# Branch-b merge gates as two sets of seven block products among the GLA key and query tiles

## The chip, the cores and the metric

One core of a Trainium2 chip runs one program. The metric is device time in microseconds (us), the median of several runs; a separate profiled run gives the trace. Engines: PE (TensorE: matmuls and transposes), ACT (ScalarE), DVE (VectorE), POOL (GpSimd) and SP (SyncE, which here only issues transfers). Weights come from DRAM by 16 DMA engines that all queues share.

## The reference, cut to what matters

256 tokens, width 2048, one layer, batch 1, all in fp32:

```python
h = rmsnorm(x, pre_norm_g)
proj = h @ w_in                     # 2048 x 18448
(a_q, a_k, a_v, a_g, a_lr, b_q, b_k, b_v, b_g, m_a, m_b) = split(proj)
gk  = log_sigmoid(a_lr @ gla_gk_w2 + gla_gk_b) / 16
o_a = rmsnorm(gla_chunked(a_q, a_k, a_v, gk), gla_norm_g) * silu(a_g)
o_b = rmsnorm(diff_attention(b_q, b_k, b_v, lam), diff_norm_g) * 0.8 * silu(b_g)
y_a, y_b = o_a @ w_branch_a, o_b @ w_branch_b
merged = sigmoid(m_a) * y_a + sigmoid(m_b) * y_b
return x + rmsnorm(merged @ w_out, post_norm_g)
```

a_q and a_k have 1024 columns, a_lr 16, all others 2048. The change is about m_b, a product of 256 x 2048 by 2048 x 2048 whose result goes through a sigmoid, and about what runs near it.

## The kernel before, in words

**Splits.** An fp32 product is made from rounded parts. Each weight tile `raw` is loaded by SP (L142) in chunks of 128 x 2048 (1 MB), and each half of it (128 x 1024) is rounded by ACT into `hi` (L161); DVE makes `lo = raw - hi` (L162). The activations have been split in the same way into `xs` (L197, L198). PE then makes three passes: x_hi w_hi, x_lo w_hi, x_hi w_lo. `raw`, `hi` and `lo` have three buffers each (L87), and `take` (L167) has halves emitted four ahead (AHEAD). So a load waits until a buffer is free, which is when DVE's `lo` has read it.

**Tiles.** The tokens are 2 blocks of 128, K is 16 tiles of 128. `token_major` (L308, matmul L322) makes 512 columns for both blocks: 16 x 2 x 3 = 96 matmuls of 512 columns, in 8 halves of 12. `channel_major` (L333) makes a k or q tile of 128 channels, in 2 halves: 16 matmuls of 512 (L343, both x parts beside one another) and 16 of 256 (L345).

**Order.** `chunk_plan` (L32) sets the order of the weights, and so that of the work: values v0 to v4, GLA keys and queries (k0, q0, k1, q1; four tiles each), GLA output gates ag0 to ag3, difference heads 0 and 1, then four times a merge gate of branch a and its branch product (m0g, y0g), heads 2 and 3, the four merge gates of branch b (m1g, L744), y1 (four), and the output product o (four). All engines' instructions are put in order at build time, under the data's dependencies.

**Tasks.** Smaller work is written as generators that `pump` (L297) advances one step every two halves: the forget gate (L368), the scores of the two halves of GLA (`gla_scores`, L454; mostly DVE and ACT), GLA's output (L554), the pairs of the difference heads (L603, L615) and the turning of the merged result (L750). The values `vh`, `vl` and the gates `gb` stay in the chip's memory until they are used; most such tiles come from one pool of 32 (L88). `merge_gate` (L721) is one `token_major` and a tanh per block: sigmoid(z) is used as (1 + tanh(z/2)) / 2. GpSimd's queue carries no transfer; the constants, w2 among them (L221), are loaded from SP's.

Of the kernel before, what the change touches and what calls it, by code (L numbers as in the profile page):

```python
# [26 lines left out]
WARM = 8  # L27
BRIDGE = 512
# [3 lines left out]
def chunk_plan():  # L32

    plan = []
    at = 0
    for g, n in enumerate(VG):
        if g == 0:
            plan.append(("v0", "two", "w_in", [(6144, RANK), (2048, 2 * n - RANK)]))
            at = 2 * n - RANK
        elif g > 1:  # L40
            plan.append((f"v{g}", "tok", "w_in", [(2048 + at, n)]))
            at += n
    for hf in range(2):
        for name, base in (("k", 1024), ("q", 0)):
            for c in range(4):
                plan.append((f"{name}{hf}{c}", "chan", "w_in", [(base + 512 * hf + P * c, P)]))
    for g in range(4):
        plan.append((f"ag{g}", "tok", "w_in", [(4096 + 512 * g, 512)]))
    o = 6144 + RANK

    def heads(g):
        plan.append((f"dv{g}", "tok", "w_in", [(o + 4096 + 512 * g, 512)]))
        plan.append((f"bg{g}", "tok", "w_in", [(o + 6144 + 512 * g, 512)]))
        for pair in range(2):
            for n, name in enumerate(("dq", "dk")):
                for c in (2 * pair, 2 * pair + 1):
                    plan.append((f"{name}{g}{c}", "chan", "w_in", [(o + 2048 * n + 512 * g + P * c, P)]))

    def gate(br, g):
        plan.append((f"m{br}{g}", "tok", "w_in", [(o + 8192 + 2048 * br + 512 * g, 512)]))  # L60

    def branch(br, g):
        plan.append((f"y{br}{g}", "tok", ("w_branch_a", "w_branch_b")[br], [(512 * g, 512)]))

    heads(0)
    heads(1)
    for g in range(4):
        gate(0, g)
        branch(0, g)
    heads(2)  # L70
    heads(3)
    for g in range(4):
        gate(1, g)
    for g in range(4):
        branch(1, g)
    for g in range(4):
        plan.append((f"o{g}", "tok", "w_out", [(512 * g, 512)]))
    return plan


@with_exitstack
def hybrid_kernel(ctx: ExitStack, tc, xt, xn, preg, postg, w, w2, gkb, glag, lamv, diffg, ident_d, causal_d, lmask_d, out):
# [5 lines left out]
    big = ctx.enter_context(tc.tile_pool(name="big", bufs=32))  # L88
    small = ctx.enter_context(tc.tile_pool(name="small", bufs=2))
    psum = ctx.enter_context(tc.tile_pool(name="psum", bufs=4, space=bass.MemoryType.PSUM))  # L90

    count = [0]
# [4 lines left out]

    def sm(shape, name, dtype=F32, bufs=2):
        count[0] += 1
        return small.tile(shape, dtype, tag=name, name=f"{name}_{count[0]}", bufs=bufs)  # L100

    def t2(shape, name):
        count[0] += 1
        return small.tile(shape, F32, tag="t2", name=f"{name}_{count[0]}", bufs=8)
# [9 lines left out]
    plan = chunk_plan()  # L114
    halves = []
    off = 0
    for key, kind, _, cols in plan:
        n = sum(c for _, c in cols)
        size = ROWS[kind] * n
        for _ in range(KT // ROWS[kind]):  # L120
            halves += [(key, off, size, 0), (key, off, size, 1)]
            off += size * P
    ready = {}
    emitted = [0]
    raws = {}

    def emit_half():
        j = emitted[0]
        emitted[0] += 1
        key, at, size, h = halves[j]  # L130
        if h == 0:
            raws[at] = wpool.tile([P, 2048], F32, tag="raw", name=f"raw_{at}")
        raw = raws[at]
        src = w[at : at + P * size].rearrange("(p n) -> p n", p=P)
# [17 lines left out]
        if key == "o3" and j + 1 < len(halves):  # L152
            hi_t, lo_t = u([P, 1024], "keep", F32R), u([P, 1024], "keep", F32R)
        else:
            hi_t = wpool.tile([P, 1024], F32R, tag="hi", name=f"hi_{j}")
            lo_t = wpool.tile([P, 1024], F32R, tag="lo", name=f"lo_{j}")
        fine = 2 if j < 2 else 1
        for i in range(fine):
            a, b = n * i // fine, n * (i + 1) // fine
            r = raw[:, n * h + a : n * h + b]  # L160
            act.activation(hi_t[:, a:b], r, AF.Copy)  # L161
            dve.tensor_tensor(out=lo_t[:, a:b], in0=r, in1=f32(hi_t[:, a:b]), op=ALU.subtract)  # L162
        ready[j] = (key, hi_t, lo_t)
# [3 lines left out]
    def take(key):  # L167
        j = used[0]
        used[0] += 1
        while emitted[0] < min(j + 1 + AHEAD, len(halves)):  # L170
            emit_half()
        name, hi, lo = ready.pop(j)
        assert name == key, (name, key)
# [38 lines left out]
    w2_raw = u([P, 1024], "w2_raw")  # L212
    w2_s = u([P, 1024], "w2_s", F32R)
    pool.memset(w2_raw, 0.0)
# [3 lines left out]
    lam_s = sm([P, 4, 64], "lam_s", bufs=1)  # L218
    def load_constants():
        for i in range(4):  # L220
            tc.keep_in_program_order(sp.dma_start(w2_raw[32 * i : 32 * i + RANK, :], w2))  # L221
# [20 lines left out]
    half_rstd = const.tile([P, 2], F32, name="half_rstd")  # L242
    rstd_bc = const.tile([P, S], F32, name="rstd_bc")
# [10 lines left out]
    def norm():  # L254
# [12 lines left out]
        dve.tensor_scalar(out=half_rstd, in0=rstd, scalar1=0.5, scalar2=None, op0=ALU.mult)  # L267

# [39 lines left out]
    def token_major(key, n, ops, step=1, groups=1):  # L308
        banks = [[ps(tag), ps(tag)] for tag in ("mm", "bg")[:groups]]
        spots = [(g, b) for g in range(groups) for b in range(2)]  # L310
        rows = 2 // groups
        for q in range(KT // rows):
            hi, lo = take(key)
            for w, parts in ((hi, (0, 1)), (lo, (0,))):
                for j in range(rows):
                    kt = rows * q + j
                    a = ops(kt)
                    for g, b in spots:
                        c = n * (groups * j + g)
                        for part in parts:  # L320
                            first, last = kt == 0 and w is hi and part == 0, kt == KT - 1 and w is lo
                            i = pe.matmul(banks[g][b][:, :n], a[part][:, P * b : P * b + P], w[:, c : c + n], start=first, stop=last)  # L322
            latest[0] = i.ins
            if groups == 1 and q % 2:
                pump(step)
            if groups == 2 and q == KT - 4:
                with tc.issue_after(latest[0]):
                    norm()
            if groups == 2 and q > 10:
                pump()  # L330
        return banks if groups == 2 else banks[0]

    def channel_major(key):  # L333
        o = ps("mm")
        for h in range(2):
            hi, lo = take(key)
            turns = [(w, j) for w in (hi, lo) for j in range(8)]
            if h:
                turns.append(turns.pop(7))
            for w, j in turns:  # L340
                kt, c = 8 * h + j, slice(P * j, P * j + P)
                if w is hi:
                    i = pe.matmul(o, hi[:, c], x_pair(kt), start=kt == 0, stop=kt == KT - 1)  # L343
                else:
                    i = pe.matmul(o[:, :S], lo[:, c], x_ops(kt)[0], start=False, stop=False)  # L345
            latest[0] = i.ins
# [12 lines left out]
    vh = [u([P, 2, 512], "vh", F32R) for _ in range(4)]  # L359
    vl = [u([P, 2, 512], "vl", F32R) for _ in range(4)]  # L360
    lr = u([P, 2, P], "lr")
    pool.memset(lr, 0.0)
    gp = [u([P, 2, 4, P], "gp") for _ in range(2)]
# [4 lines left out]
    def forget_gate():  # L368
# [6 lines left out]
        for i in (0, 64):  # L375
            act.activation(lrt[i : i + 32, :], bank[i : i + 32, :S], AF.Copy)
            r = slice(i + 32, i + 64)
            dve.tensor_tensor(out=lrt[r, :], in0=bank[r, :S], in1=f32(top[r, :S]), op=ALU.subtract)
        top = u([P, 1024], "w2h", F32R)
# [4 lines left out]
        yield  # L384
        for hf in range(2):
# [10 lines left out]
        e = [u([P, 1024], "e") for _ in range(2)]  # L396
# [12 lines left out]

    def evacuate(start, banks, n, lo):  # L410
        c0 = start
        while lo < n:
            h, c = c0 // 512, c0 % 512
            m = min(n - lo, 512 - c)
            for b in range(2):
# [3 lines left out]
                dve.scalar_tensor_tensor(out=vl[h][:, b, c : c + m], in0=src, scalar=r, in1=f32(hi), op0=ALU.mult, op1=ALU.subtract)  # L419
            lo += m  # L420
# [9 lines left out]

    def late():
# [6 lines left out]
    first_groups(token_major("v0", VG[0], x_ops, groups=2))  # L438
    tasks.append(late())
    tasks.append(forget_gate())  # L440
    start = 2 * VG[0] - RANK
    for g, n in enumerate(VG[2:]):
        banks = token_major(f"v{g + 2}", n, x_ops)
        evacuate(start, banks, n, 0)
        start += n
# [8 lines left out]
    def gla_scores(hf, q, k):  # L454
# [3 lines left out]
        suf = u([P, 2, 4, P], "suf")  # L458
        aall = u([P, 3, 2, P], "att")
        a = aall[:, :2]  # L460
        ah, al = u([P, 3, 2, P], "ath", F32R), u([P, 3, 2, P], "atl", F32R)
# [73 lines left out]
    for hf in range(2):  # L535
        ts = {}
        for name in ("k", "q"):
            ts[name] = u([P, 2, 4, P], name)
            for c in range(4):
                o, o2 = (t.rearrange("p (b t) -> p b t", b=2) for t in channel_major(f"{name}{hf}{c}"))  # L540
                bc = rstd_bc.rearrange("p (b t) -> p b t", b=2)
                t = ts[name][:, :, c, :]
                act.activation(t, o2, AF.Copy)
                dve.tensor_tensor(out=t, in0=o, in1=t, op=ALU.add)
                if name == "k":
                    dve.tensor_tensor(out=t, in0=t, in1=bc, op=ALU.mult)
                pump(1)
        tasks.append(gla_scores(hf, ts["q"], ts["k"]))


    oah = [u([P, 2, 2, S], "oah", F32R) for _ in range(4)]
    oal = [u([P, 2, 2, S], "oal", F32R) for _ in range(4)]

    def gla_out(hf, gates):  # L554
        og = []
        while f"scores{hf}" not in done:
            yield
        for h in range(2):
# [342 lines left out]
```

## Time and profile before

| | |
|---|---|
| median of 3 runs | 1140.75 us (1140.27 to 1144.84) |
| the profiled run | 1140.77 us, of which the span from first to last instruction is 1139.0 |
| PE, DVE, ACT, POOL busy | 99%, 61%, 53%, 4% of the span |
| chain that ended last | 97% PE |
| DMA | 211.60 MB, mean 186 GB/s; 176 loads of 1 MB take 4.9 us from issue to landing (median) |
| granted TensorE clock | 0.999 |

A busy share is of the span; idle time of an engine off the chain costs nothing by itself. In a row of groups, the line, engine, operation, result and operands, and shape stand before a count, then the busy time in us, the mean duration in ns, and after the second bar the idle time before these instructions and what ended it. In a row of waits, three numbers follow: us in total, times, and the longest.

### The profile page before, as it was taken

What the parts mean: (1) busy time and instruction counts of PE and PEld (TensorE: products, weight loads), DVE (VectorE), ACT (ScalarE), POOL (GpSimd) and SP (SyncE); (2) the same over time, 40 slices, a digit from 0 to 9 for tenths busy, and PEclk for the clock granted to TensorE, in tenths of its full rate; (3) what the DMA queues carried; (4) which work ended last, traced back from release to release, by engine and by line L of the source; (5) the groups of instructions that cost most, each with busy time, mean ns of one, the idle gap of its engine ahead of it and who ended that gap; (6) DMA issues with size and microseconds to landing.
All of it is one profiled execution on the core that took longest, in us unless ns stands there. A gap on an engine that the chain in (4) does not pass through costs nothing.

```text
span 1139.0 us, 14713 instructions
## 1 busy us (share of the span) xinstructions
PE 1128.4 (99%) x5690; PEld 968.5 (85%) x5690; DVE 699.8 (61%) x1027; ACT 601.4 (53%) x903; POOL 49.4 (4%) x61
## 2 busy tenths in 40 slices
PE   9999999999999999999999999999999999999997
PEld 8999888888888888888888888888888888888886
DVE  7665588657857766665554444676576544566454
ACT  7675454545646656655544434566566544444451
POOL 0100031001100000100000000000000000000000
PEclk9999999999999999999999999999999999999999
DMA  8656545555445445454555555545454555556761
GB/s 320 226 189 222 186 169 173 197 167 190 143 181 185 143 157 181 160 191 171 181 185 185 193 203 195 185 168 170 181 182 155 182 185 185 187 187 209 273 215 75
DMA packets 33174, 211.60 MB, mean 186 GB/s; under 512 B 4240, under 2 KB 5776, under 8 KB 10576
## 3 DMA queue, kind: packets, MB, share of 16 engines
q1 hardware_dynamic: 32096, 209.34, 53.0%
q10 hardware_dynamic: 1008, 1.32, 0.3%
q8 instruction: 44, 0.72, 0.2%
q14 instruction: 26, 0.21, 0.1%
HBM read 208.55 MB, written 2.10 MB: 185 GB/s over the span
## 4 chain that ended last, share of the span: by engine, by line
PE 97%; issue 1%; DMA 0%; ACT 0%; DVE 0%; SPq 0%; DVEq 0%; POOLq 0%; POOL 0%; ACTq 0%
PE mm L322 66%; PE mm L343 15%; PE mm L345 8%; PE bg L322 2%; PE mm L305 1%; PE bg L512 1%; PE bg L305 1%; PE bg L631 1%; PE bg L632 1%; PE bg L653 0%; DMA raw<-in_w_dram 0%; PE bg L662 0%; PE bg L757 0%; PE bg L663 0%; PE bg L661 0%
## 5 line engine op out<-in xcount | busy, mean ns | idle before, releaser
L162 DVE TENSOR_TENSOR lo<-raw,hi 128x1024 fp32r<-128x1024 f32 (+3 forms) x387 | 467.1, 1209 | 357.5 <-ACT hi L161 351.3
L161 ACT ACTIVATE hi<-raw 128x1024 fp32r<-128x1024 f32 (+3 forms) x387 | 401.5, 1039 | 441.2 <-PE mm L322 317.7
L322 PE MATMUL mm<-hi,xs 128*128 128x512 f32 (+2 forms) x1536 | 375.4, 386 | 0.0
L322 PEld LDWEIGHTS mm<-hi,xs 128*128 128x128 f32 x1536 | 285.0, 188 | 48.8 <-ACT hi L161 0.8
L322 PE MATMUL mm<-lo,xs 128*128 128x512 f32 (+2 forms) x768 | 201.7, 383 | 0.0
L343 PE MATMUL mm<-xs,hi 128*128 128x512 f32 x768 | 197.3, 394 | 0.0
L322 PEld LDWEIGHTS mm<-lo,xs 128*128 128x128 f32 x768 | 143.8, 188 | 25.9 <-DVE lo L162 0.3
L343 PEld LDWEIGHTS mm<-xs,hi 128*128 128x128 f32 x768 | 138.3, 189 | 24.1
L345 PEld LDWEIGHTS mm<-xs,lo 128*128 128x128 f32 x768 | 104.7, 190 | 7.6
L345 PE MATMUL mm<-xs,lo 128*128 128x256 f32 x768 | 107.1, 282 | 0.0
L322 PE MATMUL mm<-hi,obh 128*128 128x512 f32 x128 | 50.4, 394 | 0.0
L322 PE MATMUL mm<-hi,oah 128*128 128x512 f32 x128 | 50.2, 392 | 0.0
L322 PE MATMUL mm<-hi,oal 128*128 128x512 f32 x128 | 49.9, 390 | 0.0
L322 PE MATMUL mm<-hi,obl 128*128 128x512 f32 x128 | 49.9, 390 | 0.0
L642 ACT ACTIVATE prob<-prob,mx,score_scale 128x128 f32<-128x128 f32 x64 | 34.3, 537 | 24.0 <-DVE mx L637 24.0
L322 PE MATMUL mm<-hi,mh 128*128 128x512 f32 x96 | 37.5, 390 | 0.0
L322 PE MATMUL mm<-hi,ml 128*128 128x512 f32 x96 | 37.4, 389 | 0.0
L322 PE MATMUL mm<-lo,obh 128*128 128x512 f32 x128 | 34.3, 390 | 0.0
L322 PE MATMUL mm<-lo,oah 128*128 128x512 f32 x128 | 34.2, 389 | 0.0
L252 POOL TENSOR_TENSOR de<-de,neg_half 128x2 f32<-128x2 f32 x16 | 11.4, 713 | 510.4 <-DVE de L670 510.4
L322 PEld LDWEIGHTS mm<-lo,oah 128*128 128x128 f32 x128 | 24.0, 188 | 5.1
L322 PEld LDWEIGHTS mm<-lo,obh 128*128 128x128 f32 x128 | 24.0, 188 | 5.0
(195 smaller groups left out, 984.0 us busy)
## 6 DMA issues: line engine op xcount, KB each, us to landing
raw<-in_w_dram SPq DMA_DIRECT2D x176, 1024.0 KB, 4.9
raw<-in_w_dram SPq DMA_DIRECT2D x14, 832.0 KB, 6.0
raw<-in_w_dram SPq DMA_DIRECT2D x4, 800.0 KB, 4.4
xres<-in_xn_dram SPq DMA_DIRECT2D x4, 512.0 KB, 8.8
xraw<-in_xt_dram SPq DMA_DIRECT2D x3, 512.0 KB, 7.7
raw<-in_w_dram SPq DMA_DIRECT2D x3, 416.0 KB, 6.2
lmask<-in_lmask_dram SPq DMA_DIRECT2D x2, 512.0 KB, 8.6
pg<-in_postg_dram SPq DMA_DIRECT2D x2, 512.0 KB, 6.7
```

The source lines that it names most:

```text
L161: act.activation(hi_t[:, a:b], r, AF.Copy)
L162: dve.tensor_tensor(out=lo_t[:, a:b], in0=r, in1=f32(hi_t[:, a:b]), op=ALU.subtract)
L252: pool.tensor_tensor(out=dst, in0=src, in1=neg_half[:, : src.free_size()], op=ALU.pow)
L305: i = pe.matmul(out, lhs, rhs, start=first and n == 0, stop=last and n == len(pairs) - 1)
L322: i = pe.matmul(banks[g][b][:, :n], a[part][:, P * b : P * b + P], w[:, c : c + n], start=first, stop=last)
L343: i = pe.matmul(o, hi[:, c], x_pair(kt), start=kt == 0, stop=kt == KT - 1)
L345: i = pe.matmul(o[:, :S], lo[:, c], x_ops(kt)[0], start=False, stop=False)
L512: pe.matmul(o, xk[:, P * c : P * c + P], xq.rearrange("p (b c t) -> p b c t", b=2, c=4)[:, :, c, :], start=i == 0, stop=i == 1)
L631: pe.matmul(banks[m][:, lo:up], q2[:, m, i2, t], kh[:, m, i2, :n], start=True, stop=False)
L632: pe.matmul(banks[m][:, lo:up], q2[:, m, i2, t], kl[:, m, i2, :n], start=False, stop=True)
L642: act.activation(prob[m][:, lo:up], prob[m][:, lo:up], AF.Exp, scale=score_scale[:, b : b + 1], bias=mx[:, i : i + 1], accum_out=z[:, i : ...
```

## The change

The four gates of branch b are computed as two sets of 1024 columns. In a set, the two token blocks (i), the two halves of K (j) and two blocks of 512 columns make 2 x 2 blocks A_ij and B_jk, and the product A B is made from seven block products (Strassen's method, in Winograd's form) instead of eight. A block product is 8 K tiles x 3 passes = 24 matmuls of 512 columns, in 4 steps of one weight half and 6 matmuls, so a set has 168 in 28 steps.

- **Left operands.** Four sums of blocks of x are made and split once, during v2 and v3 (`sum_operands`): ACT multiplies x by the norm's gain in place (16 of 128x256), DVE makes 8 sums of 128x512, and both split four tiles of 128x1024.
- **Right operands.** Weight tiles a and b (two of each per set, t = 0 and 1) are loaded with B11 and B22 and changed in place between the products. Products come in the order 1, 3, 5, 6, 2, 7, 4. Product 1 reads a = B11; then a transfer on GpSimd's queue adds B12 to a as it lands (an accumulating DMA). Product 3 reads b = B22, product 5 reads a. For product 6 DVE adds b to a; then an accumulating transfer adds B12 to b. Product 2 reads a third tile, B21, loaded into a `raw` buffer; DVE adds it to a. Product 7 reads b, product 4 a.
- **Results.** Products 1, 6, 7 and 4 accumulate in one PSUM bank, which is read between them; the others are added by DVE. The right column block comes out negated, hence the scale `minus_half` in its tanh.
- **The mixed stretch.** After v3, `phase_steps` mixes the 56 steps of the sets with 40 other halves: v4's 8 and the 32 of k and q.
- **Moved.** The forget gate and both score tasks now start after this stretch, and run from ag0 on with two tasks pumped at a time; m00 and m01 come ahead of the heads 0; y0 follows heads 1 without gates between; m02 and m03 follow heads 3; the last tasks drain within y1's first group.
- **Kept in DRAM.** To make room, the values (8 tiles of 0.5 MB), the finished gates (4) and m00, m01 (2) are written to DRAM and fetched back later, all on GpSimd's queue; so are the four loads of w2, which were SP's. The pool of 32 becomes one of 18, and a second one of 13 takes the place of the stretch's own tiles when it is over.

Cut to its core:

```diff
+PRODUCTS = (1, 3, 5, 6, 2, 7, 4)
+BIG = 18
+MORE = 13
...
+def phase_steps():
+    keys = ["v4"] + [f"{name}{hf}{c}" for hf in range(2) for name in ("k", "q") for c in range(4)]
+    other = [(key, r, h) for key in keys for r in range(1 if key[0] in "kq" else 4) for h in range(2)]
+    steps = [("set", s, prod, t, h) for s in range(2) for prod in PRODUCTS for t in range(2) for h in range(2)]
+    mixed = []
+    for i, step in enumerate(steps):
+        mixed.append(step)
+        mixed += other[len(other) * i // len(steps) : len(other) * (i + 1) // len(steps)]
+    return mixed
...
+    def spill(t, name):
+        d = dram.tile(list(t.shape), t.dtype, name=f"{name}_{count[0]}")
+        pool.dma_start(d, t)
+        return d
+
+    def fetch(d, name, make):
+        t = make(list(d.shape), name, d.dtype)
+        pool.dma_start(t, d)
+        return t
...
+    seq = halves_of("v0", "v2", "v3") + phase_steps()
+    seq += halves_of(*(f"ag{g}" for g in range(4)), "m00", "m01") + heads_order(0) + heads_order(1)
+    seq += halves_of(*(f"y0{g}" for g in range(4))) + heads_order(2) + heads_order(3) + halves_of("m02", "m03")
+    seq += halves_of(*(f"{name}{g}" for name in ("y1", "o") for g in range(4)))
...
+    def emit_set(s, prod, t, h):
+        c = slice(1024 * h, 1024 * h + 1024)
...
+        if h == 0 and prod == 2:
+            raws[s, t] = wpool.tile([P, 2048], F32, tag="raw", name=f"raw_c_{count[0]}")
+            sp.dma_start(raws[s, t], weights(f"set{s}", 4 + t)[0])
+        a, b = chain[s, "a", t], chain[s, "b", t]
+        if prod == 6:
+            dve.tensor_tensor(out=a[:, c], in0=a[:, c], in1=b[:, c], op=ALU.add)
+        return (raws[s, t] if prod == 2 else b if prod in (3, 7) else a)[:, c]
+
+    def follow_set(s, prod, t, h):
+        c = slice(1024 * h, 1024 * h + 1024)
+        a, b = chain[s, "a", t], chain[s, "b", t]
+        if prod == 2:
+            dve.tensor_tensor(out=a[:, c], in0=a[:, c], in1=raws[s, t][:, c], op=ALU.add)
+        if h == 1 and prod in (1, 6):
+            pool.dma_start(a if prod == 1 else b, weights(f"set{s}", 2 + t)[0], accum_op=ALU.add)
...
-            act.activation(hi_t[:, a:b], r, AF.Copy)
-            dve.tensor_tensor(out=lo_t[:, a:b], in0=r, in1=f32(hi_t[:, a:b]), op=ALU.subtract)
-        ready[j] = (key, hi_t, lo_t)
+            act.activation(hi_t[:, a:b], r[:, a:b], AF.Copy)
+            dve.tensor_tensor(out=lo_t[:, a:b], in0=r[:, a:b], in1=f32(hi_t[:, a:b]), op=ALU.subtract)
+        if joined:
+            follow_set(*e[1:])
+        ready[j] = (e, hi_t, lo_t)
...
+            if c + m == 512:
+                vspill[h] = spill(vh[h], "vh"), spill(vl[h], "vl")
...
+    def block_products(s):
+        x = ps("mm")
+        bank = {1: x, 6: x, 7: x, 4: x}
+        left, right = u([P, 2, 512], "gl"), u([P, 2, 512], "gr")
...
+        for prod in PRODUCTS:
+            if prod not in bank:
+                bank[prod] = ps("mm")
+            out = bank[prod]
+            for t in range(2):
+                for h in range(2):
+                    hi, lo = take(("set", s, prod, t, h))
+                    for w, parts in ((hi, (0, 1)), (lo, (0,))):
+                        for j in range(2):
+                            kt = 4 * t + 2 * h + j
+                            a = operand(prod, kt)
+                            for part in parts:
...
+                                i = pe.matmul(out, a[part], w[:, 512 * j : 512 * j + 512], start=first, stop=last, skip_group_check=out is x)
+                    if t and h:
...
+                        if prod == 6:
+                            dve.tensor_tensor(out=right[:, 0, :], in0=x, in1=kept[3], op=ALU.add)
+                            squash(right[:, 0, :], minus_half[:, 0:1])
...
+                        if prod == 7:
+                            dve.tensor_tensor(out=right[:, 1, :], in0=x, in1=kept[5], op=ALU.add)
+                            squash(right[:, 1, :], minus_half[:, 1:2])
+                            gspill[2 * s + 1] = spill(right, "gr")
+                        if prod == 4:
+                            act.activation(left[:, 1, :], x, AF.Tanh, scale=half_rstd[:, 1:2])
+                            gspill[2 * s] = spill(left, "gl")
+                    yield
+
+    sets = (step for s in range(2) for step in block_products(s))
+    rest = others()
+    for step in phase_steps():
+        next(sets if step[0] == "set" else rest)
...
+    joint.close()
...
     tasks.append(forget_gate())
...
     for hf in range(2):
...
-                pump(1)
-        tasks.append(gla_scores(hf, ts["q"], ts["k"]))
+        tasks.append(gla_scores(hf, ts["q", hf], ts["k", hf]))
...
-        banks = token_major(f"ag{g}", 512, x_ops)
+        banks = token_major(f"ag{g}", 512, x_ops, 2)
...
+    m0 = []
+    for g in range(2):
+        t = u([P, 2, 512], "mgate")
+        merge_gate(g, lambda b: t[:, b, :])
+        m0.append(spill(t, "mgate"))
...
-    gb = [u([P, 2, 512], "gateb") for _ in range(4)]
-    for g in range(4):
-        merge_gate(1, g, gb[g])
-    while tasks:
-        pump()
+    for g in range(2, 4):
+        t = merge_gate(g, lambda b: t2([P, 512], "mgate"))
+        for b in range(2):
+            dve.scalar_tensor_tensor(out=part[g][:, b, :], in0=t[b], scalar=1.0, in1=part[g][:, b, :], op0=ALU.add, op1=ALU.mult)
+
+    gb = []
+
+    def settle():
+        while tasks:
+            pump()
+        gb.extend(fetch(d, "gateb", u) for d in gspill)
```

387 lines of the change are left out of this document (254 added, 133 removed).

## The prediction

> **What bounds the kernel now.** I read the page first: the busy shares, then the chain that ended last.
>
> ```profile
> span 1139.0 us, 14713 instructions
> PE 1128.4 (99%) x5690; PEld 968.5 (85%) x5690; DVE 699.8 (61%) x1027; ACT 601.4 (53%) x903; POOL 49.4 (4%) x61
> ...
> q1 hardware_dynamic: 32096, 209.34, 53.0%
> ...
> PE 97%; issue 1%; DMA 0%; ACT 0%; DVE 0%; SPq 0%; DVEq 0%; POOLq 0%; POOL 0%; ACTq 0%
> ```
>
> PE is busy for 99% of the span and is 97% of the chain: the time is the sum of the matmuls. The waits of PE say how little else there is:
>
> ```profile
> PE bg L240 <- DVE ones_b L237: 1.6, 1, 1.6
> PE bg L322 <- ACT hi L161: 0.7, 1, 0.7
> ```
>
> 2.3 us, all of it at the start. So a matmul taken away is worth its whole pitch, as long as every other engine and the DMA keep what they feed ahead of PE. The pitches come from the chain in order of time (start, us, piece):
>
> ```profile
> 73.05 26.53 PE mm L322 x144
> ...
> 104.95 2.07 PE mm L343 x9
> 107.02 0.95 PE mm L345 x8
> 107.97 1.61 PE mm L343 x7
> 109.58 0.95 PE mm L345 x8
> ...
> 594.16 119.73 PE mm L322 x528
> ```
>
> A 512-column matmul costs 119.73 / 528 = 0.2268 us, a 416-column one 26.53 / 144 = 0.184 (so 0.177 for 400 columns), and one k or q tile of 32 matmuls 2.07 + 0.95 + 1.61 + 0.95 = 5.58.
>
> How full DVE and the DMA may be beside a PE that doesn't wait is read from windows (length; busy us and instructions of PE, PEld, DVE, ACT, POOL; clock, DMA share, GB/s):
>
> ```profile
> 0.00:30.00 30.00, 27.73 (x132) 24.58 (x133) 21.83 (x36) 23.06 (x40) 1.43 (x7) 1.00 0.87 309
> 16.00:20.00 4.00, 4.00 (x23) 3.96 (x22) 3.93 (x8) 3.97 (x8) 0.00 (x0) 1.00 1.02 424
> 105.00:165.00 60.00, 60.00 (x343) 52.73 (x342) 38.12 (x45) 27.87 (x37) 9.11 (x6) 1.00 0.53 183
> 160.00:180.00 20.00, 20.00 (x120) 17.74 (x120) 19.90 (x30) 12.63 (x19) 0.00 (x0) 1.00 0.50 174
> ```
>
> From 160 to 180 us DVE is busy for 19.90 of 20 us, and PE loses nothing. The DMA has moved 424 GB/s; among the key and query tiles it moves 183.
>
> **The saving.** Four merge gates are 4 x 96 = 384 matmuls of 512 columns; two sets of seven products of 24 are 336. Nothing else changes on PE. 48 x 0.2268 = 10.9 us, all on the path: 1140.77 us (the profiled execution, which stands at the median, 1140.75) - 10.9 = 1129.9. What follows is what the new order may give back.
>
> **The mixed stretch.** The sets' 56 steps of 6 matmuls run among v4's 8 half tiles and the 32 halves of k and q: 336 x 0.2268 = 76.2, 96 x 0.177 = 17.0, 16 x 5.58 = 89.3; together 182.5 us of PE. What the other engines must do in it:
>
> ```profile
> L162 DVE TENSOR_TENSOR lo<-raw,hi 128x1024 fp32r<-128x1024 f32 x345 | 426.7, 1237 | 337.3 <-ACT hi L161 331.5 <-PE bg L679 4.5
> L486 DVE TENSOR_TENSOR xq<-xq,q 128x512 f32<-128x512 f32 x14 | 9.6, 685 | 0.7 <-ACT xq L485 0.7
> L162 DVE TENSOR_TENSOR lo<-raw,hi 128x800 fp32r<-128x800 f32 x8 | 7.9, 992 | 5.4 <-ACT hi L161 5.4
> L546 DVE TENSOR_TENSOR k<-k,rstd_bc 128x256 f32<-128x256 f32 x8 | 3.5, 433 | 0.2
> L544 DVE TENSOR_TENSOR k<-mm,k 128x256 f32<-128x256 f32 x8 | 3.3, 417 | 0.0
> ```
> ```profile
> L161 ACT ACTIVATE hi<-raw 128x1024 fp32r<-128x1024 f32 x345 | 365.5, 1060 | 419.6 <-PE mm L322 308.1 <-PE mm L343 95.4 <-issue 12.3
> L351 ACT ACTIVATE tanh<-mm,half_rstd 128x512 f32<-128x512 f32 x16 | 10.0, 676 | 0.0
> L197 ACT ACTIVATE xs<-xraw,preg_s 128x256 fp32r<-128x256 f32 x16 | 7.7, 496 | 0.0
> L702 ACT ACTIVATE dq<-mm 128x256 f32<-128x256 f32 x16 | 5.9, 366 | 0.0
> ```
>
> DVE: 88 splits x 1.237 + 8 x 0.992 + 16 chain additions of 128x1024 x 1.237 + 16 x 0.417 + 8 x 0.433 + 8 product sums x 0.685 + v4's evacuation (about 2) = 154 us, 84% of 182.5. ACT: 88 x 1.060 + 8 x 0.9 + 16 x 0.366 + 12 copies and tanh of 128x512 x 0.676 + 2 = 116 us. Neither fills it. Locally products 6 and 2 have an addition beside every split: per step DVE has 2 x 1.237 + 40/56 x 1.237 + 0.2 = 3.56 us against PE's 1.36 + 40/56 x 2.66 = 3.26. Over the 4 steps of a product DVE falls 1.2 us behind, and 3 split buffers (one per 1.9 us of PE) hold 5.7 us. Moreover a DVE instruction costs less than its duration when the next is ready:
>
> ```profile
> 161.08 1.22 DVE L162 TENSOR_TENSOR lo<-raw,hi 128x1024 fp32r<-128x1024 f32 x1
> 162.22 0.69 DVE L495 TENSOR_TENSOR xk<-xk,k 128x512 f32<-128x512 f32 x1
> ```
>
> 1.14 from start to start where 1.22 is the duration. By that, 3.56 becomes 3.3: even. I cost the additions at 0, and 4 x 1.2 = 5 us if the cover is gone.
>
> The operand sums, made during v2 and v3, add 8 x 0.685 + 4 x 1.237 = 10.4 us to DVE and 16 x 0.25 to 0.5 + 4 x 1.06, some 12 at most, to ACT, over 36 us of PE in which DVE stood at about two thirds (38.12 of 60 in the later window): 0, at most 2.
>
> **The accumulating transfers.** Eight of 1 MB go from GpSimd's queue into the weight tiles a and b in place. Before has none, and no transfer on that queue; the nearest rows:
>
> ```profile
> raw<-in_w_dram SPq DMA_DIRECT2D x176, 1024.0 KB, 4.9
> raw<-in_w_dram SPq DMA_DIRECT2D x14, 832.0 KB, 6.0
> ...
> xres<-in_xn_dram SPq DMA_DIRECT2D x4, 512.0 KB, 8.8
> ...
> lmask<-in_lmask_dram SPq DMA_DIRECT2D x1, 128.0 KB, 10.0
> ```
>
> Bounds: 4.9 us (a plain 1 MB load), and 3 x 8.8 = 26 if the memory is gone over three times in a crowd. Slack: tile a is last read in product 1 and next in product 5, seven set steps later, 7 x 3.26 = 22.8, less the first split's 1.06: about 21 us. On its queue a spill of 2 x 0.5 MB stands ahead of the second tile's. I take 12 us (twice the busy 6.0), so 0; at 26 us it costs 5 per set, 10 in all. The Trainium skill ("DMA: Bandwidth & Descriptors", the anatomy of one DMA) fits a GpSimd transfer with 2.0 us + bytes / 436 GB/s; by that, as an estimate, a plain 1 MB takes 4.4 us and the sum is the same. It gives no figure for accumulating ones.
>
> All traffic of the stretch: sets 20 MB, v4 3.2, k and q 16, spills about 6: 45 x 1.049 = 47 MB in 182.5 us, 259 GB/s, or 303 if an accumulation counts twice. That is well below 424, but above 183, so landings get longer.
>
> **The load chain of product 2.** SP issues a load when a raw buffer comes free:
>
> ```profile
> SPq L142 <- DVE lo L162: 878.8, 171, 8.5
> ```
>
> Product 2 puts its third operand into one of the same three raw buffers and holds it until its addition. Followed along the order of after's instructions, a split frees a buffer, the operand lands (4.9), is added behind a split, two more splits follow, the next k tile lands (4.9) and is split: it is ready within a us of when PE needs it. So every us of landing above 4.9 counts about twice, once per set: 0 at 4.9, 2 x 2.2 = 4.4 at 6.0, 2 x 7.8 = 15.6 at 8.8. Most k loads here stand alone, as the 4.9 row does; I take 0.7 per set, 1.4.
>
> **Smaller steps.** Product 4 writes the PSUM bank that DVE must read after product 7; other matmuls of the order stand between, about 0.3 x 2 = 0.6. Both score tasks now run at once from the gates of a on: some 51 us of DVE against 47 of PE for the same 17 half tiles by the durations, covered as at 160 to 180: 0.7, at most 4. Values fetched back (8 x 0.5 MB on GpSimd's queue) are issued, by the order of the steps, some 20 us before PE's first use; four of them take 8.8 in the row above, eight 17.6: 0, at most 3. The first branch-b gate is fetched two half tiles (5.4 us) before DVE adds it, and DVE's splits are 3 tiles (8 us) ahead, so it may land in 13 us: 0. Heads 3's steps now drain in 8 pumps of two under m02 and m03 and in y1, where they had 16: 0. The release of the first pool, before whose end the forget gate can't begin: 0.3.
>
> Sum: 1129.9 + 1.4 + 0.6 + 0.7 + 0.3 = 1132.9.
>
> **Rivals.**
> (1) DVE and landings give most of it back. For: DVE at 84% with 3.56 against 3.26 us in products 6 and 2, and the product 2 chain at zero margin. Against: 160 to 180 us. Landings of 6.0 (4.4) and half the additions' cover gone (2.5) on top of 1.5 small: 1129.9 + 8.4 = 1138.3.
> (2) Slower: the accumulating transfers land late. PE stands until tile a is there, once per set. Above 21 us each us counts twice; with the 3 us of the sum, 1146.4 is reached at a landing of 21 + (1146.4 - 1132.9) / 2 = 27.8 us, just beyond my bound of 26; at 32 us it would be 1132.9 + 22 = 1155. For: no such transfer was ever seen here, and it reads what it adds to. Against: four to five times the plain row. The Trainium skill ("TensorE: Matmul & The Clock Gate", the clock gate) has PE's clock halved after some 3.4 us of idling and for as long after it resumes: as an estimate, 1.7 us more per such gap, so 1158. No row of before has such a gap (the longest wait is 1.6 us, clock 1.00), so the trace cannot say.
> (3) The saving isn't there: with a new weight tile per 1.36 us instead of 2.72, PE waits for splits throughout, and the stretch runs at its feeders' pace, 1140.8. Against: 96 splits x 1.237 is 119 of 182.5 us.
>
> **The numbers.** Forecast 0.54 (1130 to 1135), rival 1 0.20, rival 2 and like mishaps beyond 1146.4 0.22, rival 3 0.04. Half a per cent, 1135.0 and 1146.4, is about what a measurement can tell from no change. Rival 1 reaches down below 1135 for a fifth: faster 0.58, same 0.20, slower 0.22. Range: 1129.5 (nothing given back) to 1150, which takes in rival 1, the 26 us bound and the near part of rival 2.
>
> **What would show it.** In the profile after: PE busy near 1117 and its waits below 5 us; the 1 MB accumulations landing below 21 us; DVE at 80 to 90% in the mixed stretch; PE's longest wait behind product 2's loads. Wrong, if PE's waits name the accumulating transfer, if they sum up to over 15 us, or if the clock falls below 1.00.

## The result and the profile after

The changed kernel takes 1149.89 us (median; 1149.34 to 1150.34) where the kernel before takes 1140.80: the ratio is 1.0072 (95% interval 1.0048 to 1.0095). It is slower by 9 us, at the upper edge of the range, where 1133 and a gain were forecast. The profiled execution took 1149.55 us, its span 1147.7.

From the page of the changed kernel:

```profile
span 1147.7 us, 14888 instructions
PE 1127.6 (98%) x5642; PEld 961.2 (84%) x5642; DVE 761.0 (66%) x1088; ACT 640.9 (56%) x957; POOL 71.6 (6%) x101
...
PEclk9999999989999999999999999999999999999998
...
q0 software_dynamic: 5312, 23.33, 7.5%
...
PE 93%; DMA 3%; ACT 1%; DVE 1%; issue 1%; DVEq 0%; SPq 0%; POOLq 0%; POOL 0%; ACTq 0%
```

PE has 48 matmuls fewer, worth 10.9 us, and yet is busy for 1127.6 us instead of 1128.4. So most of what was saved is lost inside busy time: matmuls have become slower. A second part is in the chain, where 3% is now DMA, and in the ninth slice of the clock, which reads 8 (the last slice does so too, but PE's work ends there). The waits of PE, and those of DVE and ACT that stand behind them:

```profile
PE bg L429 <- DVE lo L232: 6.5, 2, 4.3
PE bg L308 <- DVE ones_b L305: 1.6, 1, 1.6
PE bg L427 <- ACT hi L231: 1.2, 3, 0.6
PE bg L390 <- ACT hi L231: 0.9, 1, 0.9
```
```profile
DVE keep L232 <- PE mm L375: 10.9, 1, 10.9
DVE a L186 <- DMA raw_c<-in_w_dram: 10.5, 3, 6.2
```

Two waits of PE, 6.5 us together, are for a `lo` that DVE makes. DVE at that time stands before the addition of product 2 (L186), whose operand `raw_c` has not landed. The other DVE wait, 10.9 us for a `keep` tile, is at the very end of the kernel. The DMA groups:

```profile
raw<-in_w_dram SPq DMA_DIRECT2D x160, 1024.0 KB, 5.0
...
a<-in_w_dram POOLq DMA_DIRECT2D x4, 1024.0 KB, 11.1
b<-in_w_dram POOLq DMA_DIRECT2D x4, 1024.0 KB, 8.6
raw_c<-in_w_dram SPq DMA_DIRECT2D x4, 1024.0 KB, 8.6
```

The accumulating transfers land in 11.1 and 8.6 us, in good time for their own readers. It is a plain load, `raw_c`, that is late, at 8.6 against 5.0.

**Where the slower matmuls are.** Pieces of the chain of the changed kernel in order of time (start, us, piece): a gate group ag, a y0 group and a y1 group.

```profile
299.64 54.43 PE mm L407 x240
...
640.19 11.20 PE mm L407 x48
...
973.79 16.80 PE mm L407 x72
```

54.43 / 240 = 0.2268 us as before the change; 11.20 / 48 and 16.80 / 72 are 0.2333. The same y0 matmuls stood in the 0.2268 row of the kernel before. Taken over all of y0 and y1 (768 matmuls) that is 768 x 0.0065 = 5.0 us; with the products of the operand sums (192), the GLA output's and the last output tile's it is some 7 us.

The account against the span before: 1139.0 - 10.9 + 7 (slower matmuls) + 8 (waits: 8.6 against 0.7, without the start's 1.6) + 2.3 (half clock: it lasts until 235.7 us, 4.6 us of that after PE has gone on; the windows stand near the end of this text) + 1.5 (the end) is 1146.9, and 1147.7 was measured. The last 0.8 us is not assigned.

### The profile page after: what moved, and what is told of

Its sections match the earlier page's. It is cut to its first block, busy times and chain, and to the rows that moved or that the text cites. A ratio compares the mean times of both kernels' runs of the same rounds, so it can differ in the third digit from the quotient of the medians.

```text
span 1147.7 us, 14888 instructions
## 1 busy us (share of the span) xinstructions
PE 1127.6 (98%) x5642; PEld 961.2 (84%) x5642; DVE 761.0 (66%) x1088; ACT 640.9 (56%) x957; POOL 71.6 (6%) x101
## 4 chain that ended last, share of the span: by engine, by line
PE 93%; DMA 3%; ACT 1%; DVE 1%; issue 1%; DVEq 0%; SPq 0%; POOLq 0%; POOL 0%; ACTq 0%
PE mm L407 55%; PE mm L427 10%; PE mm L648 5%; PE mm L429 5%; PE bg L427 4%; PE bg L429 2%; DMA raw_c<-in_w_dram 2%; PE bg L390 2%; PE mm L375 2%; PE mm L390 2%; PE bg L407 1%; PE bg L748 1%; DMA raw<-in_w_dram 1%; PE bg L375 1%; PE bg L859 1%
## 5 line engine op out<-in xcount | busy, mean ns | idle before, releaser
L232 DVE TENSOR_TENSOR lo<-raw,hi 128x1024 fp32r<-128x1024 f32 (+3 forms) x355 | 428.6, 1209 | 271.8 <-ACT hi L231 268.9
L407 PE MATMUL mm<-hi,xs 128*128 128x512 f32 (+1 forms) x1152 | 283.4, 388 | 0.0
L407 PEld LDWEIGHTS mm<-hi,xs 128*128 128x128 f32 x1152 | 213.2, 188 | 37.8
L407 PE MATMUL mm<-lo,xs 128*128 128x512 f32 (+1 forms) x576 | 151.6, 385 | 0.0
L427 PE MATMUL mm<-xs,hi 128*128 128x512 f32 x512 | 132.8, 394 | 0.0
L427 PEld LDWEIGHTS mm<-xs,hi 128*128 128x128 f32 x512 | 92.3, 189 | 16.1
L427 PE MATMUL bg<-xs,hi 128*128 128x512 f32 x256 | 66.9, 392 | 1.2 <-ACT hi L231 1.2
L427 PEld LDWEIGHTS bg<-xs,hi 128*128 128x128 f32 x256 | 48.1, 189 | 11.8 <-ACT hi L231 2.0
L232 DVE TENSOR_TENSOR lo<-a,hi 128x1024 fp32r<-128x1024 f32 x32 | 38.7, 1223 | 15.9 <-ACT hi L231 14.5
L429 PE MATMUL bg<-xs,lo 128*128 128x256 f32 x256 | 36.7, 287 | 6.5 <-DVE lo L232 6.5
## 6 DMA issues: line engine op xcount, KB each, us to landing
a<-in_w_dram POOLq DMA_DIRECT2D x4, 1024.0 KB, 11.1
```

Source lines behind the costliest of these rows:

```text
L232: dve.tensor_tensor(out=lo_t[:, a:b], in0=r[:, a:b], in1=f32(hi_t[:, a:b]), op=ALU.subtract)
L407: i = pe.matmul(banks[b][:, :n], a[part][:, P * b : P * b + P], w[:, n * j : n * j + n], start=first, stop=last)
```

## The experiments

**The address of a tile: three experiments.** What y0, y1 and the sums have in common is that their stationary tiles lie in the two new pools. In the addresses of the built program all tiles of the kernel before start at the same place modulo 512 bytes in the weight buffers and in the large pool. In the changed kernel the new constant `minus_half` (8 bytes, padded to 32) moves every pool by 32 bytes, off a 64-byte boundary, and the tiles that precede them put the operand sums 64 bytes and y0's and y1's operands 320 bytes (modulo 512) away from the weight halves they are multiplied with. So there are two theories: the boundary, or the distance.

```diff
     minus_half = const.tile([P, 2], F32, name="minus_half")
+    shift = const.tile([P, 8], F32, name="shift")
+    pool.memset(shift, 0.0)
```

> The changed kernel with one more constant tile of 32 bytes, so that every pool moves up by 32 bytes and all tiles start at 0 modulo 64 bytes, as before the change; the distances between pools stay. In the changed kernel the 512-column matmuls whose stationary tile is in the new pools (y0, y1, the operand sums) start 233 ns apart, those with the stationary tile in the old pool 227. Absolute theory (a tile off a 64-byte boundary is slow): the 233 become 227, some 1040 matmuls x 6.5 ns = 6.8 us, time about 1143. Relative theory (what counts is the distance between the stationary and the moving tile modulo 512 bytes): no change, 1149.9, pitch 233.

Measured: 1149.64 us, ratio to the kernel before 1.0070 (1.0055 to 1.0085). Nothing changed, so the boundary is not it.

```diff
+    gap = pools[0].tile([P, 112], F32, tag="gap", name="gap", bufs=1)
+    pool.memset(gap, 0.0)
...
     pools[0] = ctx.enter_context(tc.tile_pool(name="small", bufs=2))
+    gap = pools[0].tile([P, 48], F32, tag="gap", name="gap2", bufs=1)
+    pool.memset(gap, 0.0)
```

> The changed kernel with a pad of 448 bytes in the stretch's own pool and one of 192 bytes in the pool that follows it, so that the operand sums and the tiles of y0 and y1 lie at the same place modulo 512 bytes as the weight halves they are multiplied with (they were 64 and 320 off); everything stays off a 64-byte boundary by 32. Relative theory: pitch 227 everywhere, 6.8 us less, about 1143. Absolute theory: no change, 1149.9. The waits of PE (8.6 us) stay in both.

Measured: 1145.55 us, ratio 1.0032 (1.0020 to 1.0045): 4.3 us less, by two pads. In the trace y0's and y1's matmuls are back at a median of 227 ns. The waits are as they were. The gain is short of 6.8. In this profile the first weights were 1.5 us late at the start, where the changed kernel's profile has 0.9, and a half clock of 3.4 us stands there that the other lacks. And the products of the sums came down only from 233 to 230 ns on average. That rest has nothing to do with the pads: in this trace the second to sixth matmul after a change from another group come 231 ns apart on average and the seventh to twelfth 227, and the sets' products of x itself, whose tiles no pad moved, do the same. Why the first ones after a change are slower is open.

The third takes the kernel before and only puts the distance in:

```diff
+    gap_pool = ctx.enter_context(tc.tile_pool(name="gap", bufs=1))
     big = ctx.enter_context(tc.tile_pool(name="big", bufs=32))
+    gap = gap_pool.tile([P, 16], F32, name="gap")
+    nc.gpsimd.memset(gap, 0.0)
```

> The kernel before with 64 bytes put between the weight buffers and the large pool, nothing else: all tiles stay on 64-byte boundaries, but activations and weights are no longer at the same place modulo 512 bytes. Relative theory: the 2976 matmuls of 512 columns of the token-major groups go from 227 to 233 ns, 19 us, and the narrower and channel-major ones may too, up to 7 more: 1158 to 1167. Absolute theory, or any cause in the changed kernel's traffic: no change, 1140.8.

Measured: 1157.33 us, ratio 1.0138 (1.0123 to 1.0153), 16 us for 64 unused bytes. The chain of this kernel has the same piece that gave the pitch in the prediction:

```profile
118.27 2.07 PE mm L346 x9
...
601.86 123.20 PE mm L325 x528
...
1126.35 10.96 PE mm L308 x48
```

123.20 / 528 = 0.2333 where it was 119.73 / 528 = 0.2268. The token-major matmuls of 512 columns pay 6.5 ns each in this row and some 18 us in all, near the 19 expected. The 768 channel-major ones of 256 columns became quicker, 117 ns for 119, so the total stayed just below the range that was written down.

The distance is the cause. It is not the place as such: in the addresses of the built programs x stands at 320 modulo 512 bytes here, as it does in the first of the three experiments, where the weights stand at 320 too and x's matmuls are quick (227 ns). And the last output tile's matmuls (L308), whose two operands both lie in the shifted pool, take 10.96 us for 48 where it was 10.89. But the rule is narrower than the theory: in the k and q tiles the weight half is stationary and x moves, at the same 64 bytes, and nine matmuls of 512 columns (L346) take 2.07 us as before. The cost is shown for an activation as the stationary tile only.

**Product 2: what makes its operand late.** In the changed kernel, DVE and PE around the longer wait (start, us, instruction, idle time before and who ended it):

```profile
221.28 1.22 DVE L186 TENSOR_TENSOR a<-a,raw_c 128x1024 f32<-128x1024 f32 x1
228.70 1.23 DVE L186 TENSOR_TENSOR a<-a,raw_c 128x1024 f32<-128x1024 f32 x1 [6.20 <-DMA raw_c<-in_w_dram]
229.84 1.22 DVE L232 TENSOR_TENSOR lo<-raw,hi 128x1024 fp32r<-128x1024 f32 x1
```
```profile
224.79 1.99 PE L427 MATMUL bg<-xs,hi 128*128 128x512 f32 x8
231.12 2.07 PE L429 MATMUL bg<-xs,lo 128*128 128x256 f32 x8 [4.33 <-DVE lo L232]
```

The split that PE waits for is of a k tile that has long been there; it stands on DVE behind an addition whose operand is missing. That operand's load was issued at 217.3 and took 11.3 us. The DMA view of the stretch from 215.5 to 222 us (queue: packets, MB, share of 16 engines; then the issues), and of 109 to 115 us in the first set:

```profile
q0 software_dynamic: 112, 0.92, 80.3%
q1 hardware_dynamic: 10, 0.08, 3.1%
...
b<-in_w_dram POOLq DMA_DIRECT2D x1, 1024.0 KB, 9.0
raw_c<-in_w_dram SPq DMA_DIRECT2D x1, 1024.0 KB, 11.3
```
```profile
q0 software_dynamic: 128, 1.05, 96.6%
```

q0 is GpSimd's queue. 1 MB of accumulation holds the 16 engines for nearly 6 us, at 175 GB/s, and SP's queue q1 moves next to nothing in that time (its `raw_c` was issued at 111.9 us in the first set). The first attempt was to let `raw_c` go first:

```diff
-        if h == 1 and prod in (1, 6):
+        if h == 1 and (prod == 1 or prod == 6 and t == 0):
             pool.dma_start(a if prod == 1 else b, weights(f"set{s}", 2 + t)[0], accum_op=ALU.add)
+        if (prod, t, h) == (2, 1, 0):
+            seen = pool.tensor_copy(sm([P, 2], "seen", bufs=1), raws[s, 1][:, :2])
+            with tc.issue_after(seen.ins):
+                pool.dma_start(b, weights(f"set{s}", 3)[0], accum_op=ALU.add)
```

> The changed kernel, but the accumulating transfer into the second tile b of each set is queued behind a tiny GpSimd copy out of the third operand's second tile, so it starts only when that tile has landed. Theory of the feeder (the accumulating transfer keeps the load queue off the DMA engines, the third operand lands 8.7 and 11.3 us after its issue, DVE stands before its addition with the split that PE needs behind it): PE's waits for splits, 6.5 us, and the half clock after the longer one, 3.4 us, go: about 1140. Rival (the load is late because its buffer is freed late, or because of the spills): under 3 us gained, 1147 to 1150. A second rival: the late tile b now holds up product 7, and the wait only moves: 1145 to 1155.

Measured: 1149.28 us, ratio 1.0070 (1.0055 to 1.0085). The old wait is gone and a new one has come, as the second rival had it, though not at product 7. (By the number alone the first rival fits as well; that the old wait is gone speaks against it.) ACT and PE in the first set, 8 us later than the old wait:

```profile
137.64 1.06 ACT L235 ACTIVATE hi<-raw 128x1024 fp32r<-128x1024 f32 x1 [4.12 <-DMA raw<-in_w_dram]
```
```profile
138.75 3.23 PE L431 MATMUL bg<-xs,hi 128*128 128x512 f32 x8 [2.91 <-ACT hi L235]
```

Now it is the next k tile's load that stands behind the accumulation. So it is not this load's place alone: whichever load meets the accumulation comes late, and PE waits. That the three raw buffers, which set when a load is issued, leave no slack for it is my reading; no run with more buffers was made.

Next, the accumulation left out, in two ways: all eight as plain loads of the same bytes, or those into b not at all (in both, sums are left out and the branch-b gates come out otherwise).

```diff
-            pool.dma_start(a if prod == 1 else b, weights(f"set{s}", 2 + t)[0], accum_op=ALU.add)
+            pool.dma_start(a if prod == 1 else b, weights(f"set{s}", 2 + t)[0])
```

> The changed kernel with the eight accumulating transfers made plain loads of the same bytes into the same tiles from the same queue (the sums in a and b are left out, so the gates come out otherwise). In the changed kernel a packet of 8 KB takes 630 ns where it accumulates and about 240 to 320 where it is a plain load; one accumulating transfer fills the engines for 5 us, and loads that were issued behind it move nothing until it ends. Theory (it is the accumulation that holds up the loads): PE's waits fall from 8.6 us below 2.5, the clock stays at 1.00, 9 to 11 us gained: 1139 to 1141. Rival (any 1 MB on GpSimd's queue in that place does it, or too few raw buffers by themselves): under 4 us gained, 1146 or more.

Measured: 1144.46 us, ratio 1.0034 (1.0022 to 1.0046), a gain of 5.4: between the two expectations.

```profile
PE bg L429 <- DVE lo L232: 2.8, 2, 1.5
PE bg L427 <- ACT hi L231: 1.8, 4, 0.7
PE bg L308 <- DVE ones_b L305: 1.6, 1, 1.6
PE bg L390 <- ACT hi L231: 1.2, 1, 1.2
PE mm L390 <- ACT hi L231: 0.5, 1, 0.5
```

The waits for a `lo` are less than half, 2.8 us for 6.5, and the clock is whole in the stretch. But all waits beside the start's (1.6) only fall from 8.6 to 6.3 us, where below 2.5 was expected, and `raw_c` still takes 6.8 us. So the accumulation is part of the matter, and a plain 1 MB in that place costs something too: in the first set 1.5 us of the 2.2 are left.

```diff
-        if h == 1 and prod in (1, 6):
+        if h == 1 and prod == 1:
             pool.dma_start(a if prod == 1 else b, weights(f"set{s}", 2 + t)[0], accum_op=ALU.add)
```

> The changed kernel without the four accumulating transfers into b (the sum in b is left out, the gates come out otherwise); those into a stay. Both long waits of PE come in product 2, right behind b's transfers. Theory: PE's waits below 2.5 us, 1139 to 1141. If the transfers into a hold up loads just as much, waits of 3 us or more appear elsewhere and the time is above 1143.

Measured: 1140.74 us, ratio 1.0003 (0.9993 to 1.0014). 9.2 us come back: no wait of PE for a `lo` is left, `raw_c` lands in 5.2 us, and the only half clock left is after PE's last matmul. The transfers into a, at 12.0 us, cost nothing. What then keeps this kernel from 1130 is the 7 us of slower matmuls, the end, and 2 us more of small waits than before the change.

In the second set this run also took away something else. The four small loads of w2 (`w_raw`), which the change moved to GpSimd's queue, go out in the changed kernel right behind the second accumulation into b, in the same two microseconds as the late `raw_c`; here they went out 35 us earlier. First the changed kernel's row, then this run's, then the queues of the changed kernel from 222 to 229 us, when the accumulation is all but over and `raw_c` still lands:

```profile
217.31 1.97 POOL L470 DMA_DIRECT2D w_raw<-in_w_dram  x4 [0.30 <-POOL w_raw L468]
```
```profile
182.18 1.98 POOL L470 DMA_DIRECT2D w_raw<-in_w_dram  x4 [0.30 <-POOL w_raw L468]
```
```profile
q1 hardware_dynamic: 134, 0.97, 47.4%
q0 software_dynamic: 160, 0.39, 23.9%
```

So the wait of 2.2 us in the first set, where no such load is near, is shown to come from the transfers into b. Of the 4.3 us in the second set, some 3 are the accumulation's: with plain loads and w2's loads still in that place (217.6 us) 1.3 were left. Whether these 1.3 are the plain megabyte or w2's loads was not tested.

**Two mends for the waits.** One keeps everything and cuts each accumulation in four:

```diff
-            pool.dma_start(a if prod == 1 else b, weights(f"set{s}", 2 + t)[0], accum_op=ALU.add)
+            dst, src = a if prod == 1 else b, weights(f"set{s}", 2 + t)[0]
+            for n in range(0, 2048, 512):
+                pool.dma_start(dst[:, n : n + 512], src[:, n : n + 512], accum_op=ALU.add)
```

> The changed kernel with each accumulating transfer of 1 MB cut into four of 128x512 on the same queue; bytes and results are the same. If an engine changes from queue to queue only between whole transfers, a load now waits for one quarter (1.3 us) and not for 5 us: PE's waits below 4 us, the clock whole, 1139 to 1144. Rival (the engines' total time counts, not the order): waits stay at 6 to 9 us, 1147 to 1151; smaller packets may even add to it.

Measured: 1146.02 us, ratio 1.0048 (1.0033 to 1.0063): 3.9 us gained, less than expected. `raw_c` still takes 8.5 us, PE's waits are 5.5 us beside the start's, and the half clock after them shrinks from 6.8 to 3.4 us. The load was not let in between the quarters: it was issued at 111.1 us in the first set, and from 109 to 114 us the queues moved

```profile
q0 software_dynamic: 521, 0.94, 112.3%
...
q1 hardware_dynamic: 1, 0.00, 0.0%
```

What became better is the latest of the four `raw_c`, 8.8 us to landing for 11.3; why, is open. With the pads:

> Quarters and the pads of the second experiment together. If both theories hold the gains add: 4.3 us by the pads and 6 to 10 by the quarters, 1135 to 1140, below the kernel before. If the quarters do nothing: 1145.5.

Measured: 1141.57 us, ratio 1.0004 (0.9994 to 1.0014). The two gains, 4.3 and 3.9, add up to the 8.3 measured; the kernel is level with the one before.

The other mend deals the halves out anew, so that products 6 and 2 take longer:

```diff
+    share = [4 if step[2] in (6, 2) else 2 for step in steps]
     for i, step in enumerate(steps):
         mixed.append(step)
-        mixed += other[len(other) * i // len(steps) : len(other) * (i + 1) // len(steps)]
+        mixed += other[len(other) * sum(share[:i]) // sum(share) : len(other) * sum(share[: i + 1]) // sum(share)]
```

> The changed kernel with the 40 other halves dealt out otherwise: 1.11 behind each step of products 6 and 2, 0.56 behind each step of the other products (0.71 behind each before). PE then takes 4.3 us per step of products 6 and 2, not 3.3, so the same 10 us of accumulating transfers and the loads of the third operand have a third more time. If the waits come from the crowd in that place: PE's waits for splits (6.5 us) and the half clock (3.4 us) go, 1139 to 1143. Rival (the additional k tiles need raw buffers and loads of their own in that place, so the wait stays): 1147 to 1152. A second one: products 1, 3 and 5 are now too quick for the transfer into a (11 us in 19): a new wait there.

Measured: 1143.90 us, ratio 1.0025 (1.0016 to 1.0034), 6.0 us gained, just short of what the theory said. The first set no longer waits; in the second one wait is left:

```profile
PE bg L430 <- DVE lo L233: 3.2, 1, 3.2
```

and 6.8 us of half clock around it. It is again the set in which w2's loads go out beside `raw_c` (206.3 and 207.8 us).

**The end.** The 10.9 us in which DVE stood before a `keep` tile:

```profile
1118.10 0.68 DVE L1043 TENSOR_TENSOR yg<-mm,pg 128x512 f32<-128x512 f32 x1
1129.73 1.23 DVE L232 TENSOR_TENSOR keep<-raw,keep 128x1024 fp32r<-128x1024 f32 x1 [10.95 <-PE mm L375]
```

Token block 0's last part is made behind it, at 1134 to 1138, and block 1's behind that. From PE's last matmul to the end of the span it takes 9.6 us, before the change 8.1.

```diff
-MORE = 13
+MORE = 14
...
-            make = u if e[1:] == (3, 0) else u2
-            hi_t, lo_t = make([P, 1024], "keep", F32R), make([P, 1024], "keep", F32R)
+            hi_t, lo_t = u2([P, 1024], "keep", F32R), u2([P, 1024], "keep", F32R)
```

> The changed kernel with all 14 kept splits of the last output tiles in the pool of late tiles, made 14 instead of 13. In the changed kernel one of them waits 10.9 us for a tile that PE still reads; DVE stands there, and the last part of token block 0 comes out behind it, 16 us later in the end than before the change; the end after PE's last matmul takes 9.6 us where it took 8.15. Expected if that order is the cause: 1.4 us less, 1148.5. Rival: the end is as long, 1149.9.

Measured: 1149.27 us, ratio 1.0068 (1.0053 to 1.0083). The order is right again in the trace and its end takes 8.6 us, 1.0 less. The 0.6 us in the medians is inside their spread, so that the whole kernel gains by it is not shown. (The 16 us in the expectation is not in the traces: block 0's last part starts at 1134.7 us where it was 1120.2, which is 14.5 us by the clock and 7 us when counted from PE's last matmul.)

**All of it together.**

> The pads of the second experiment, the dealing out and the kept splits together. If the three parts are separate, their gains add: 4.3 + 7 to 10 + 1.4 from 1149.9, 1134 to 1137, which is below the kernel before. If the waits stay: 1144.

Measured: 1137.88 us, ratio 0.9977 (0.9968 to 0.9986). Expected were 1134 to 1137; as in the experiment with the halves alone, one wait of 3.4 us is left in the second set.

> The same with the accumulating transfers in quarters as well. If the dealing out alone has taken the waits away, quarters add nothing (within 1 us of the one without); if some wait is left, 1 to 3 us less.

Measured: 1135.53 us, ratio 0.9946 (0.9930 to 0.9963), 5.3 us quicker than the kernel before.

```profile
PE bg L433 <- DVE lo L236: 1.8, 1, 1.8
PE bg L312 <- DVE ones_b L309: 1.6, 1, 1.6
PE bg L394 <- ACT hi L235: 1.2, 1, 1.2
PE mm L652 <- DVE gr L668: 0.4, 1, 0.4
PE mm L394 <- ACT hi L235: 0.4, 1, 0.4
```

The remaining wait no longer halves the clock in the stretch. So the saving of the seven products was real: with the same arithmetic, by a change of places and of the order, two thirds of the forecast gain (5.3 of 7.9 us) are there.

## Why the prediction was wrong

Two steps failed: "Nothing else changes on PE", which cost 7 us, and the 1.4 us for the load chain of product 2, which measured 6.5 us of waits and 2.3 us of half clock. With 1.5 us at the end these are 16 of the 17 us between 1132.9 and 1149.9.

- **The saving, 10.9 us.** Right as to matmuls: 48 fewer, and with the places and the order changed the time does fall. Wrong in "Nothing else changes on PE": the pitch of 0.2268 was taken for every 512-column matmul, those of y0, y1 and the operand sums among them. They take 0.2333. I read the pitch from one row of before and held it for a property of the shape; it depends on where two tiles lie. This is 7 us, and no term of the sum or bound allowed for it.
- **The mixed stretch.** DVE's load cost nothing, as said, and was less than forecast: from 83 to 276 us it is busy for 145 of 193 us, 75% and not 84. No wait of PE in the changed kernel is for an addition as such (with the halves dealt out anew one of 0.4 us is, for the sum of a product), and without the transfers into b the same additions stood beside no wait for a `lo`. Products 6 and 2 were the right place to look at, but for the DMA.
- **The accumulating transfers.** Their landing was taken as 12 us with a slack of 21; measured 11.1 and 8.6, and nobody waited for their result. What was missing is that only their own readers were asked. The bytes were counted as traffic (303 GB/s against 424; by its own terms it should be 305), an average that says nothing of engines which one transfer holds for nearly 6 us.
- **The load chain of product 2.** This was the term: the working gave 2 us for each microsecond of landing above 4.9, and the 8.8 row gave 7.8 per set. The load landed at 8.7 and 11.3, and the value taken, 0.7 per set, came from the argument that loads stand alone there. It measured 2.2 and 4.3 us of waits, 6.5 together, and 2.3 us more through the clock: the term was 7 us too small, because the two paragraphs were not put together. The place was right, the path only in part: not a second landing made PE wait but DVE, which stood before the addition with the split of a k tile behind it that had long landed. By the rule of 2 us for each, 8.7 and 11.3 would have cost 7.6 and 12.8; so the rule was too dear, and the landing that it was fed with too early.
- **Smaller steps.** The bank of product 4, the score tasks, the values fetched back (10.8 to 12.1 us to landing), the fetched gates: none shows as a wait of more than 0.9 us. The end was not looked at; it was longer by 1.5 us in the profile.
- **The rivals.** The slower one was priced for the transfer's own readers and did not happen so. What happened is rival 1's mechanism (landings) with nobody's 7 us of pitch on top. That 1149.9 still lies below the 1150 at the range's end is luck: this end was drawn for an accumulating transfer that its readers wait for. The Trainium skill's rule ("TensorE: Matmul & The Clock Gate", the HAM clock gate) that a pause halves the clock came true: 2.1 us into the 4.3 us wait the clock falls to 0.50, for 6.8 us, and PE's next group of 256 columns took 2.07 us where it took 1.11.

```profile
228.00:229.00 1.00, 0.00 (x0) 0.00 (x0) 0.30 (x1) 0.00 (x0) 0.00 (x0) 0.93 0.01 4
229.00:230.00 1.00, 0.00 (x0) 0.00 (x0) 1.00 (x2) 0.00 (x0) 0.00 (x0) 0.50 0.00 0
...
234.00:235.00 1.00, 1.00 (x4) 0.81 (x3) 1.00 (x1) 0.07 (x1) 0.00 (x0) 0.50 0.69 98
235.00:236.00 1.00, 1.00 (x4) 0.76 (x4) 1.00 (x3) 1.00 (x2) 0.00 (x0) 0.65 0.62 188
```

(windows of the changed kernel; the clock is the third number from the end.) The threshold of 3.4 us is not what the runs show: a wait of 1.8 us in the run with quarters and one of 2.2 us in the run of the kept splits were followed by a halved clock of 3.4 us each, one of 2.2 us in the first set of the changed kernel by none.

Open: what distances other than 64 and 320 bytes cost, why the k and q tiles don't pay for 64, and what w2's loads alone would cost.

## What to carry to other kernels

When a kernel is bound by PE, compare the pitch of the same matmul in both profiles before looking for waits: a tile of a few bytes, put between two pools, can move operands against each other and cost more than the arithmetic saves (16 us here, against 10.9). Ask of a new transfer not only when it lands but what cannot move while it does; and when several loads can meet it, moving one of them only moves the wait. Two costs that were each bounded in their own paragraph can be cause and effect.

## What was not expected of the hardware

A 128x512 fp32 matmul with an activation as its stationary tile and a weight half moving takes 226.8 ns from start to start when the two tiles start at the same place modulo 512 bytes, and 233.3 ns when they are 64 or 320 bytes apart; 64 bytes in front of a pool cost 16 us in the kernel before. With the weight half stationary, 64 bytes cost nothing. An accumulating transfer of 1 MB into the chip's memory moves 175 GB/s, less than half of the 424 that loads reach here, and meanwhile another queue's load, issued behind it, moves nothing.
